# Splitting the weights of an encoder kernel by two GpSimd DMAs instead of by ScalarE and VectorE

## The chip, the core and the metric

The kernel runs on one core of a Trainium2 chip. TensorE (PE in the profile) multiplies matrices out of SBUF into PSUM; VectorE (DVE), ScalarE (ACT) and GpSimd (POOL) work elementwise; SyncE (SP) issues transfers between HBM and SBUF, and GpSimd can issue them as well. Each engine works through its own queue in order and waits on semaphores that other engines and transfers raise. The metric is the device time of one launch in microseconds; lower is better.

## What is computed

One inference step of a hybrid encoder of two layers, for a prompt of 512 columns and a sample of 64, both with the same weights, in float32:

```python
for l in range(DEPTH):                                   # DEPTH = 2, D_MODEL = 1024, D_FF = 2816
    x = x + 0.5 * ((silu(h @ w_gate) * (h @ w_up)) @ w_down)     # h = rms_norm(x), first feed-forward
    u = rms_norm(x) @ w_in                               # three groups of heads: band, differential, latent
    x = x + concat(A, B, C) @ w_out                      # softmax mixers with per-head RMS norms
    x = x + memory_attention(rms_norm(x), k, v)          # k, v from 256 memory tokens: mem_w_k, mem_w_v
    x = x + 0.5 * ((silu(h @ w_gate) * (h @ w_up)) @ w_down)     # second feed-forward
```

The outputs are both groups' x and the new keys, values and latents of each layer.

## The kernel before

Activations stand transposed, 128 features by 576 columns (512 of the prompt and 64 of the sample), worked on in two halves of 288. To keep float32 accuracy with the fast matrix format, each operand is split into a rounded part, hi, and a remainder, lo = value - hi; a product is three matmuls, hi x hi, hi x lo and lo x hi. For the weights these parts are the tiles `whi` and `wlo`, 128 rows by up to 512 columns.

All weights lie in one array `wf` in the order of their use, cut into units of up to 1024 columns. `take` (line 575) fetches the next unit: `fetch` lets SyncE load it into a buffer `stage`, and `parts` splits it in pieces of 512 columns: `whi` is rounded by ScalarE or VectorE (`hi`, line 524), and `wlo` is `stage` less `whi` on VectorE (`split2`, line 543). `rows2` (line 596) takes two units at once for a form of seven products of half the size: of its seven weight operands three are `stage` itself and four are sums `wc` made of it, and all seven go through `parts`.

A feed-forward layer has 22 row tiles of gate and up. The first 4 run singly (tiles `g`, `u`), the others in pairs by `rows2` (products `P`); the down products (`d`) of a chunk of tiles stand amid the pairs of the next chunk, three, three and two of them behind each pair, and the last eight at the end. A down unit of six blocks is two weight tiles, of 512 and 256 columns. Then come the input projections (`pj`, `cq`, `ckv`, `uq`, `ukv`) mixed with attention (scores `S`, maps `p`, transposes `T`, outputs `O`), keys and values of the memory (`mk`, `mv`), the output projection (`wo`), the memory's queries (`mq`) and output (`mo`), and the second feed-forward layer.

The order of all this isn't written by hand. `Program` records every instruction with a cost per engine, `order` runs a list scheduler over them (per engine the instruction that can start first among the 24 of highest priority, within the buffers at hand), and `issue` (line 387) emits them; all instructions therefore have line 401 in the profile. An instruction that may run on several engines goes to the one that the planner's model finishes first on. The time of a matmul in that model is `n / 2.4 + 3` ns for n columns. Weights have a priority ahead of their use by up to 9.9 us (`ahead`). Buffers: 49 of 576 columns, 11 of 896, 3 stages, 6 each for `whi` and `wlo`.

Of the kernel before, what the change touches and what calls it, by code (L numbers as in the profile page):

```python
# [49 lines left out]
def ffn_steps():  # L50
    """Gate and up, the first row tiles singly and the others in pairs; the down products of a chunk amid the next one's."""
# [98 lines left out]
class Tile:  # L150
    """A tile of the recorded program; it gets its place when the ordered program is issued."""
# [68 lines left out]
class Op:  # L220
    __slots__ = ("calls", "costs", "prio", "deps", "users", "wait", "need", "tiles", "ends", "start", "extra", "done", "port")


class Program:
    """Records instructions, orders them by a model of the engines, then issues them in that order."""

    def __init__(self):
# [8 lines left out]
        self.reach = {"s": (-12000.0, 3000.0), "b": (-12000.0, 4000.0)}  # L236
# [6 lines left out]
    def op(self, costs, calls, outs, ins, extra=0.0):  # L243
        o = Op()
        sb = sum(1 for v in ins if isinstance(v, View) and v.tile.tag != "sm" and v.size() > 1)
# [29 lines left out]
    def order(self, slots, window=60000.0, depth=24):  # L275
# [43 lines left out]
        while len(out) < len(self.ops):  # L319
# [52 lines left out]
            if e == "SP":  # L372
                dma = max(end + 650.0, dma) + o.extra
                o.extra = dma + 900.0 - end
                end = dma + 900.0
# [44 lines left out]
class Trunk:  # L420
    N_S = 49
    N_B = 11
    STAGE = 3
    WB = 6
# [27 lines left out]
    def mms(self, items):  # L452
        """One uninterrupted run of matrix products: (out, lhsT, rhs, start, stop, transpose)."""
        cost, calls, outs, ins = 0.0, [], [], []
        for out, lhsT, rhs, start, stop, tr in items:
# [4 lines left out]
            elif rhs.dtype == F32:  # L460
                cost += 2 * max(2 * n / 2.4, 107) + 6
            else:
                cost += max(n / 2.4 + 3, 60 if lhsT is self.lastw else (107 if m > 64 else 60))
# [54 lines left out]
    def load(self, out, src):  # L518
        self.p.op({"SP": 475.0}, [("dma_start", dict(out=out, in_=src))], [out], [], out.size() * 4 * out.shape[0] / 360.0)

    def store(self, dst, src):
        self.p.op({"SP": 475.0}, [("dma_start", dict(out=dst, in_=src))], [], [src], src.size() * 4 * src.shape[0] / 360.0)
# [51 lines left out]

    def take(self):
        """The next unit of the weights: loaded, and split into two parts that one pass each carries."""
        p = self.p
        keep, p.shift = p.shift, self.ahead()
        st, u = self.fetch()
        n = UNIT_COLS[u]  # L580
        hl = [self.parts(st[:, c:min(n, c + 512)]) for c in range(0, n, 512)]
# [14 lines left out]
    def rows2(self):  # L596
        """Two row tiles of the next weights times self.xc in seven products of half the size (Winograd's form)."""
# [894 lines left out]
```

## Time and profile before

| what | value |
|---|---|
| median of 3 runs | 2457.14 us (2455.83 to 2457.31) |
| span of the profiled execution, first to last instruction | 2453.7 us |
| busy share of PE, VectorE, ScalarE, GpSimd | 99%, 81%, 54%, 8% |
| moved by DMA | 224.19 MB, of it 208.33 MB read from HBM |
| granted clock of TensorE, mean | 1.000 |

The profiled execution's time around its span is not listed; its span stands 3.4 us under the median of the runs. Matmuls are pipelined and their ends are modelled: one of 288 columns is shown as 0.29 us long while the next begins 0.13 us after it. So the busy share of PE says more than the engine does, and the number of matmuls in a stretch, or the distance of their starts, tells how full it is.

### The profile page before, as it was taken

What the parts mean: (1) busy time and instruction counts of PE and PEld (TensorE: products, weight loads), DVE (VectorE), ACT (ScalarE), POOL (GpSimd) and SP (SyncE); (2) the same over time, 40 slices, a digit from 0 to 9 for tenths busy, and PEclk for the clock granted to TensorE, in tenths of its full rate; (3) what the DMA queues carried; (4) which work ended last, traced back from release to release, by engine and by line L of the source; (5) the groups of instructions that cost most, each with busy time, mean ns of one, the idle gap of its engine ahead of it and who ended that gap; (6) DMA issues with size and microseconds to landing.
All of it is one profiled execution on the core that took longest, in us unless ns stands there. A gap on an engine that the chain in (4) does not pass through costs nothing.

```text
span 2453.7 us, 46432 instructions
## 1 busy us (share of the span) xinstructions
PE 2427.7 (99%) x18150; PEld 2392.1 (97%) x18150; DVE 1978.0 (81%) x4044; ACT 1326.7 (54%) x2682; POOL 202.9 (8%) x187
## 2 busy tenths in 40 slices
PE   8999999999999999999999999999999999999999
PEld 8999999999989999999999999999999999999999
DVE  8987776689886898887688877776898868987774
ACT  6544445679765644443454444465897556444442
POOL 1000000022020010000020000000211101100000
PEclk9999999999999999999999999999999999999999
DMA  4232233122332123222323232331223421223322
GB/s 146 95 98 82 89 110 121 63 72 76 117 126 74 52 83 99 90 81 93 100 70 99 85 102 82 111 114 61 74 93 104 130 69 62 78 93 93 93 82 94
DMA packets 77452, 224.19 MB, mean 91 GB/s; under 512 B 8880, under 2 KB 13040, under 8 KB 77232
## 3 DMA queue, kind: packets, MB, share of 16 engines
q1 hardware_dynamic: 77232, 221.23, 27.8%
q8 instruction: 142, 2.33, 0.4%
q14 instruction: 78, 0.64, 0.1%
HBM read 208.33 MB, written 12.86 MB: 90 GB/s over the span
## 4 chain that ended last, share of the span: by engine, by line
PE 92%; DVE 5%; ACT 2%; issue 1%; DMA 0%; SPq 0%; DVEq 0%; ACTq 0%
PE P L401 32%; PE d L401 23%; PE pj L401 7%; PE wo L401 4%; PE g L401 4%; PE u L401 4%; PE mq L401 2%; PE mo L401 2%; PE O L401 2%; PE st L401 2%; PE cq L401 2%; DVE p L401 1%; PE ckv L401 1%; PE S L401 1%; PE T L401 1%; PE OS L401 1%
## 5 line engine op out<-in xcount | busy, mean ns | idle before, releaser
L401 ACT ACTIVATE whi<-stage 128x512 fp32r<-128x512 f32 (+1 forms) x609 | 362.9, 597 | 502.9 <-PE P L401 188.5
L401 DVE TENSOR_TENSOR wlo<-stage,whi 128x512 fp32r<-128x512 f32 (+1 forms) x706 | 460.8, 662 | 130.5 <-ACT whi L401 113.4
L401 PE MATMUL d<-hhi,wlo 128*128 128x288 f32 x1408 | 415.0, 295 | 0.0
L401 PE MATMUL d<-hhi,whi 128*128 128x288 f32 x1408 | 414.9, 295 | 0.0
L401 PE MATMUL d<-hlo,whi 128*128 128x288 f32 x1408 | 414.7, 295 | 0.0
L401 ACT ACTIVATE whi<-wc 128x512 fp32r<-128x512 f32 x284 | 179.4, 633 | 327.3 <-PE d L401 171.2
L401 DVE TENSOR_TENSOR wlo<-wc,whi 128x512 fp32r<-128x512 f32 x288 | 198.3, 690 | 91.4 <-ACT whi L401 87.3
L401 PEld LDWEIGHTS d<-hhi,wlo 128*128 128x128 f32 x1408 | 264.1, 188 | 0.0
L401 PEld LDWEIGHTS d<-hhi,whi 128*128 128x128 f32 x1408 | 264.1, 188 | 0.0
L401 PEld LDWEIGHTS d<-hlo,whi 128*128 128x128 f32 x1408 | 264.1, 188 | 0.0
L401 PE MATMUL P<-xbl,whi 128*128 128x288 f32 x864 | 254.2, 294 | 0.4 <-DVE xbl L401 0.4
L401 PE MATMUL P<-xbh,wlo 128*128 128x288 f32 x864 | 254.5, 295 | 0.0
L401 PE MATMUL P<-xbh,whi 128*128 128x288 f32 x864 | 254.0, 294 | 0.0
L401 PE MATMUL pj<-xhi,whi 128*128 128x288 f32 x576 | 172.0, 299 | 0.0
L401 PE MATMUL P<-xsl,whi 128*128 128x288 f32 x576 | 169.7, 295 | 0.6 <-DVE xsl L401 0.6
L401 PE MATMUL P<-xsh,wlo 128*128 128x288 f32 x576 | 169.7, 295 | 0.1
L401 PE MATMUL P<-xrh,wlo 128*128 128x288 f32 x576 | 169.8, 295 | 0.0
L401 PE MATMUL pj<-xhi,wlo 128*128 128x288 f32 x576 | 169.8, 295 | 0.0
L401 PE MATMUL P<-xrl,whi 128*128 128x288 f32 x576 | 169.7, 295 | 0.0
L401 PE MATMUL P<-xsh,whi 128*128 128x288 f32 x576 | 169.7, 295 | 0.0
L401 PE MATMUL pj<-xlo,whi 128*128 128x288 f32 x576 | 169.6, 295 | 0.0
L401 PE MATMUL P<-xrh,whi 128*128 128x288 f32 x576 | 169.6, 294 | 0.0
(415 smaller groups left out, 6897.5 us busy)
## 6 DMA issues: line engine op xcount, KB each, us to landing
stage<-wf SPq DMA_DIRECT2D x269, 512.0 KB, 3.5
stage<-wf SPq DMA_DIRECT2D x100, 384.0 KB, 3.0
stage<-wf SPq DMA_DIRECT2D x40, 256.0 KB, 2.7
o_k<-ev SPq DMA_DIRECT2D x12, 288.0 KB, 2.1
o_v<-ev SPq DMA_DIRECT2D x12, 288.0 KB, 2.7
cache<-ckv SPq DMA_DIRECT2D x12, 256.0 KB, 3.9
x<-x SPq DMA_DIRECT2D x8, 288.0 KB, 5.7
o_y<-x SPq DMA_DIRECT2D x8, 288.0 KB, 2.1
```

The lines of the kernel that those rows point to most:

```text
L401: getattr(eng[e], fn)(**{n: real(v) for n, v in k.items()})
```

## The change

Weights outside the seven-product form (all but the very first unit, which keeps the old path) are no longer staged. GpSimd issues a DMA from `wf` into `whi`, which rounds on the way because the target is the fast format (`cast`); ScalarE writes the negative of `whi` into `wlo`; and GpSimd issues a second DMA from the same place of `wf`, which adds to `wlo` (`gather`). So each such weight is read from HBM twice, and VectorE has no part in it. 388 tiles of 512 and 100 of 256 columns go this way; the 216 `stage` operands of `rows2` and its 288 `wc` stay. The priority of a cast is 3 us further ahead than that of the rest of its unit.

With it come other numbers: 8 instead of 6 buffers each for `whi` and `wlo`, 2 instead of 3 stages, 47 instead of 49 general buffers; a limit on how early the tags `hi` and `lo` may be taken; 2048 instead of 256 bytes for the descriptors of GpSimd's DMAs; and the planner's matmul cost, now `0.4375 * n + 7`, 133 ns for 288 columns where it was 123. All engines' orders are made anew by that.

```diff
-        self.reach = {"s": (-12000.0, 3000.0), "b": (-12000.0, 4000.0)}
+        self.reach = {"hi": (0.0, 4500.0), "lo": (0.0, 4500.0), "s": (-12000.0, 3000.0), "b": (-12000.0, 4000.0)}
...
-    N_S = 49
+    N_S = 47
     N_B = 11
-    STAGE = 3
-    WB = 6
+    STAGE = 2
+    WB = 8
...
-                cost += max(n / 2.4 + 3, 60 if lhsT is self.lastw else (107 if m > 64 else 60))
+                cost += max(0.4375 * n + 7, 60 if lhsT is self.lastw else (109 if m > 64 else 60))
...
+    def cast(self, out, src):
+
+        self.p.op({"POOL": 1000.0}, [("dma_start", dict(out=out, in_=src))], [out], [], out.size() * 4 * out.shape[0] / 360.0, True)
+
+    def gather(self, out, src):
+
+        self.p.op({"POOL": 1000.0}, [("dma_start", dict(out=out, in_=src, accum_op=ALU.add))], [out], [out],
+                  out.size() * 8 * out.shape[0] / 360.0, True)
...
+    def loaded_parts(self, src, n):
+
+        hi, lo = self.new("hi", [128, 512], F32R, "whi"), self.new("lo", [128, 512], F32R, "wlo")
+        self.p.shift -= self.EARLY
+        self.cast(hi[:, :n], src)
+        self.p.shift += self.EARLY
+        self.act(lo[:, :n], hi[:, :n], AF.Copy, scale=-1.0)
+        self.gather(lo[:, :n], src)
+        return hi, lo
+
+    EARLY = 3000.0
+
...
-        st, u = self.fetch()
-        n = UNIT_COLS[u]
-        hl = [self.parts(st[:, c:min(n, c + 512)]) for c in range(0, n, 512)]
+        u = self.unit
+        if u:
+            self.unit += 1
+            n = UNIT_COLS[u]
+            src = self.a["wf"][int(UNIT_OFF[u]):int(UNIT_OFF[u + 1])].rearrange("(p c) -> p c", p=128)
+            hl = [self.loaded_parts(src[:, c:min(n, c + 512)], min(n - c, 512)) for c in range(0, n, 512)]
+        else:
+            st, u = self.fetch()
+            n = UNIT_COLS[u]
+            hl = [self.parts(st[:, c:min(n, c + 512)]) for c in range(0, n, 512)]
...
-    nc = _bacc.Bacc("TRN2", target_bir_lowering=False, num_devices=1, dynamic_dma_scratch_size=256)
+    nc = _bacc.Bacc("TRN2", target_bir_lowering=False, num_devices=1, dynamic_dma_scratch_size=2048)
```

Three places show how the orders move. The first is ScalarE at the start of the program, before (`x_66` is the first tile of x):

```order
L401 ACT_TABLE_LOAD
L401 ACTIVATE accsq<-x_66 128x576
L401 ACTIVATE xhi<-x_66,gains 128x576
L401 ACTIVATE xhi<-x_74,gains 128x576
L401 ACTIVATE sq<-x_74 128x576
```

And ScalarE at the same place after the change (`x_68` is the first tile of x):

```order
L402 ACT_TABLE_LOAD
L402 ACTIVATE wlo<-whi 128x512
L402 ACTIVATE accsq<-x_68 128x576
L402 ACTIVATE xhi<-x_68,gains 128x576
L402 ACTIVATE wlo<-whi 128x512
```

Two negations of weights now stand around the first work on x; each waits for a cast to land.

The second is the queue that loads weights amid the pairs and down products of the first feed-forward layer: SyncE's before (1024 columns are a unit of `rows2`, 512 and 768 a down unit).

```order
L401 DMA stage<-wf 128x1024
L401 DMA stage<-wf 128x512 x3
L401 DMA stage<-wf 128x1024 x4
L401 DMA stage<-wf 128x512 x3
L401 DMA stage<-wf 128x1024 x4
```

GpSimd's queue there after the change, casts (`whi`) and additions (`wlo`):

```order
L402 DMA whi<-wf 128x512
L402 DMA wlo<-wf 128x512
L402 DMA whi<-wf 128x512 x2
L402 DMA wlo<-wf 128x512 x2
L402 DMA whi<-wf 128x512 x3
L402 DMA wlo<-wf 128x512 x3
L402 DMA whi<-wf 128x512 x2
L402 DMA wlo<-wf 128x512 x2
L402 TENSOR_TENSOR wc<-stage 128x512
```

The down units' loads have moved from SyncE to GpSimd, two for each tile, and an addition stands behind all the casts of its group; SyncE keeps the units of `rows2`.

The third is VectorE amid attention in the first layer, behind the split of a sample's transposed map (`ptsl`), before:

```order
L401 TENSOR_TENSOR ptsl<-TS,pts 64x128
L401 TENSOR_TENSOR ptsl<-TS,pts 128x256
L401 TENSOR_TENSOR ev<-pj,rb 128x288
L401 SCALAR_TENSOR_TENSOR ev<-ev,gains,sqf 128x576
L401 TENSOR_TENSOR vlo<-cache,vhi 128x256
L401 TENSOR_TENSOR qlo<-ev,qhi 128x576
L401 COPY qbd_769<-qhi 64x64
L401 COPY qbd_771<-qlo 64x64 x2
L401 TENSOR_TENSOR wlo<-stage,whi 128x512
L401 SCALAR_TENSOR_TENSOR ev<-ev,gains,sqf 128x576
L401 TENSOR_TENSOR ev<-pj,rb 128x288
L401 TENSOR_TENSOR wlo<-stage,whi 128x512
```

VectorE at a like place after the change:

```order
L402 TENSOR_TENSOR ptsl<-TS,pts 64x128
L402 TENSOR_TENSOR ptsl<-TS,pts 128x256
L402 TENSOR_TENSOR sql<-sqf,sqh 128x576
L402 TENSOR_TENSOR vlo<-cache,vhi 128x256
L402 SCALAR_TENSOR_TENSOR ev<-ev,gains,sqf 128x576
L402 TENSOR_TENSOR qlo<-ev,qhi 128x576
L402 TENSOR_TENSOR ev<-pj,rb 128x288
L402 COPY qbd_724<-qlo 64x64 x2
L402 TENSOR_TENSOR ev<-pj,rb 128x288
L402 TENSOR_TENSOR sqf<-ev 128x576
```

The subtractions of weights have gone from the queue, and squares and their remainders (`sqf`, `sql`), which ScalarE or GpSimd had in part before, stand there instead.

## Rows read from the trace of the kernel before

**Rows 1.** The page's first part: busy time and share of each engine.

```profile
span 2453.7 us, 46432 instructions
...
PE 2427.7 (99%) x18150; PEld 2392.1 (97%) x18150; DVE 1978.0 (81%) x4044; ACT 1326.7 (54%) x2682; POOL 202.9 (8%) x187
```

**Rows 2.** The page's fourth part, the chain that ended last: shares by engine.

```profile
PE 92%; DVE 5%; ACT 2%; issue 1%; DMA 0%; SPq 0%; DVEq 0%; ACTq 0%
```

**Rows 3.** Timeline, start and end: start, length, instruction, idle time before it.

```profile
5.55 0.43 DVE L401 CAST whi<-stage 128x512 fp32r<-128x512 f32 x1 [4.55 <-DMA stage<-wf]
...
6.13 0.58 PE L401 MATMUL g<-xhi,whi 128*128 128x288 f32 x1 [6.13 <-DVE whi L401]
...
2449.72 0.29 PE L401 MATMUL d<-hhi,wlo 128*128 128x288 f32 x1
```

**Rows 4.** Table of stretches: engines' busy us (instructions), TensorE's clock, DMA share.

```profile
50.00:100.00 50.00, 48.88 (x365) 48.18 (x364) 48.98 (x99) 24.92 (x45) 6.10 (x10) 1.00 0.30 94
100.00:150.00 50.00, 50.00 (x380) 50.00 (x378) 41.89 (x79) 23.30 (x41) 0.00 (x0) 1.00 0.31 101
400.00:450.00 50.00, 50.00 (x373) 48.82 (x372) 34.59 (x90) 32.89 (x74) 4.44 (x6) 1.00 0.28 96
...
500.00:700.00 200.00, 193.85 (x1417) 182.15 (x1416) 182.34 (x481) 168.29 (x408) 41.16 (x42) 1.00 0.28 93
1750.00:1950.00 200.00, 193.85 (x1454) 184.22 (x1454) 184.04 (x489) 159.93 (x398) 43.41 (x40) 1.00 0.31 102
```

**Rows 5.** TensorE's waits (its weight loads): releaser, us in total, times, longest.

```profile
PEld T L401 <- DVE p L401: 4.6, 7, 0.8
...
PEld st L401 <- DVE sql L401: 3.3, 10, 0.7
PEld TS L401 <- ACT ps L401: 2.7, 5, 1.1
```

**Rows 6.** Timeline of TensorE in attention, one stop.

```profile
518.11 0.30 PE L401 MATMUL st<-sqh,onesr 96*96 96x288 f32 x1
518.86 0.38 PE L401 MATMUL st<-sql,onesr 96*96 96x288 f32 x1 [0.45 <-DVE sql L401]
```

**Rows 7.** Groups by shape: busy us, mean ns of one | idle.

```profile
L401 DVE TENSOR_TENSOR wlo<-stage,whi 128x512 fp32r<-128x512 f32 x606 | 421.0, 702 | 114.6 <-ACT whi L401 97.6
...
L401 ACT ACTIVATE whi<-stage 128x512 fp32r<-128x512 f32 x511 | 321.9, 631 | 433.0 <-PE P L401 129.6 <-issue 99.9 <-PE d L401 55.9
...
L401 DVE CAST whi<-stage 128x512 fp32r<-128x512 f32 x95 | 42.7, 452 | 19.6 <-PE pj L401 7.7 <-DMA stage<-wf 4.5 <-PE mq L401 3.5
L401 DVE TENSOR_TENSOR wlo<-stage,whi 128x256 fp32r<-128x256 f32 x100 | 42.1, 421 | 15.8 <-ACT whi L401 15.8
...
L401 POOL CAST cqs<-qhi 128x64 fp32r<-128x64 f32 x4 | 8.0, 1989 | 11.0 <-ACT qhi L401 11.0
```

**Rows 8.** Stretches again, instructions on wlo alone, then on whi or wlo.

```profile
500.00:700.00 200.00, 85.89 (x291) 53.65 (x290) 29.38 (x41) 1.00 0.28 93
...
50.00:100.00 50.00, 48.64 (x244) 38.87 (x242) 16.83 (x25) 14.05 (x23) 1.00 0.30 94
500.00:700.00 200.00, 119.11 (x582) 92.46 (x582) 37.76 (x59) 14.57 (x24) 1.00 0.28 93
```

**Rows 9.** DMA: MB and share of 16 engines; issues, KB, median us to landing.

```profile
q1 hardware_dynamic: 77232, 221.23, 27.8%
...
stage<-wf SPq DMA_DIRECT2D x40, 256.0 KB, 2.7
...
cache<-ckv SPq DMA_DIRECT2D x12, 256.0 KB, 3.9
x<-x SPq DMA_DIRECT2D x8, 288.0 KB, 5.7
...
cst<-cckv SPq DMA_DIRECT2D x2, 256.0 KB, 5.9
```

**Rows 10.** Chain from 695 to 705 us: start, length, instructions.

```profile
701.39 3.24 PE mv L401 x27
```

## What I expect of the change

> **What bounds the kernel now.** I read the page's busy shares first. TensorE (PE) is busy 2427.7 of 2453.7 us, VectorE 81%, ScalarE 54%, GpSimd 8% [rows 1]; the chain of work that ended last is 92% PE [rows 2]. So whatever is taken off the vector engines is worth something only where PE waits for them. Span less PE busy is 26.0 us. 6.1 of that is the wait before the first matmul [rows 3], and 3.7 lies behind the last one, which ends at 2450.0 [rows 3], while the output is stored; 16.2 us are waits inside. Next, the table of stretches [rows 4]: from 100 to 150 us, in the feed-forward layer, PE is full, 380 matmuls in 50 us or 131.6 ns each. The stretch from 50 to 100 us holds 365, with VectorE at 48.98 of 50. The two attention stretches, 500 to 700 and 1750 to 1950 us, show PE at 193.85 of 200 each, so 12.3 of the 16.2 us are there; VectorE is at 182 to 184 and ScalarE at 160 to 168 of 200. The list of PE's waits names softmax maps and squares late from VectorE or ScalarE first, no weight tile among its longest [rows 5]. A wait also costs more than it shows, since matmul ends are modelled: in [rows 6] two matmuls start 0.75 us apart where 0.13 would do, so 0.62 us is lost and 0.45 is shown. The hidden 0.17 us comes with each stop, and stops are mostly 0.3 to 1.1 us, so I take the true loss inside at up to twice the shown one, some 30 us. That is the ceiling of any gain inside.
>
> **What VectorE and ScalarE lose and get.** Counted in the two orders, 488 weight tiles (388 of 512 columns, 100 of 256) leave the old path. VectorE loses 388 subtractions at 702 ns and 100 at 421 ns [rows 7], 272.4 + 42.1 = 314.5 us, and 91 of 95 roundings at 452 ns, 41 us. The planner gives it back some of GpSimd's work (28 sums of wc, at about the 702 ns of a subtraction 20 us, and a few smaller), so VectorE should end near 1978 - 315 - 41 + 30 = 1650 us, 67%. ScalarE no longer rounds 297 wide and 98 narrow tiles, but negates all 488: 91 wide ones more at 631 ns [rows 7], about +58 us, near 56%. PE's matmuls are the same in number and shape. In the saturated stretches all of this is worth nothing.
>
> **Where PE waits, what it is worth.** From 500 to 700 us VectorE spends 29.4 us on weights' low parts and another 8.4 us on roundings (the row of whi or wlo less that of wlo) [rows 8]. There VectorE and ScalarE together go from 350.6 of 400 us to 350.6 - 37.8 + 11.7 (some 18 negations more at 631 ns) = 324.5, so their free time grows from 49 to 75 us, by half. If waits for a late vector engine fall as its queue has half again as much room, a third of them goes: of 24.6 us in both attention stretches (12.3 shown, doubled) 8 us. From below this could be 0 (the waits are the length of the softmax chain itself, which is not shortened), from above all 24.6. I take 8, since the longest waits in [rows 5] are of both sorts. From 50 to 100 us, 15 matmuls are missing, 15 x 0.1316 = 2.0 us, behind a VectorE that is full, with 16.8 us of it on low parts [rows 8]: gone, -2. From 400 to 450 us 7 matmuls are missing [rows 4], 0.9 us, and the 50 us behind it lack as many, beside the first work of attention: -2, with 0 as the other end.
>
> **The start.** ScalarE's second instruction is now a negation that waits for the first cast. Before, the first matmul at 6.13 waits for the rounding of the first tile, which begins at 5.55 [rows 3]. A cast issued at about 0.8 us and landing as the 256 KB loads do, in 2.7 to 5.9 us [rows 9], is there at 3.5 to 6.7; negation, square and scaled x (some 0.65 each, 2.1 in all) then end at 5.6 to 8.8 against 6.13: a delay of 0 to 2.7 us. Five casts and three additions also share the DMA engines with x, whose loads already take 5.7 us [rows 9]. I take +2, with 0 and +5 as ends.
>
> **The chain that has to stay hidden.** A weight tile now needs cast, negation, addition in turn, and each waits on the one before. No row shows a GpSimd DMA. Each leg is bounded below by 2.7 us (256 KB loads of SP beside little else) and above by 5.9 (the slowest such load) [rows 9]; the addition also reads its target, so its upper end is twice that, 11.8. With a negation of 0.63 the chain is 6.0 to 18.3 us. I take 3.9 (the median of the loads amid attention) + 0.63 + 5.3 = 9.8. It is covered by eight slots: a cast can go out when PE frees the slot eight tiles back, and seven tiles of PE work stand between. Where a run of products P gives way to down products, those seven are 12 matmuls each, 7 x 12 x 0.1316 = 11.1 us; counted in the new order, the 224 down tiles have 11.4 to 21 us. 9.8 is within it, by little, so it costs nothing. One rule speaks here: the Trainium skill (DMA: Bandwidth & Descriptors, Anatomy of one DMA) gives a GpSimd DMA about 2.0 us plus its bytes at 436 GB/s, 2.6 us for 256 KB; by it the chain would be about 6 to 7 us and the sum unchanged. No run shows that yet.
>
> GpSimd's own queue has 976 DMAs. In-order, an addition that waits for ScalarE holds the later casts, and PE waits for those. The tightest place is memory keys, memory values and output projection: 32 tiles, 64 DMAs, against 16 x 12 x 0.120 us (27 matmuls in 3.24) [rows 10] + 16 x 24 x 0.1316 = 73.5 us of PE, and a lead of seven wide tiles, 22 us, so 95 us in all: 1.5 us for each DMA. GpSimd's slowest elementwise row is 2.0 us [rows 7], the upper end, nothing the lower; I take 1.0, the middle, since no tile passes through the engine here, which fits. The DMA engines: 221 MB took 27.8% [rows 9], so 256 KB takes 0.81 us of them; a cast plus an addition at twice that is 2.4 us, where PE uses a 512-column tile in 3.16. It fits as well, and would not if the addition ran at a third of the copy's rate.
>
> **Sum.** -8 - 2 - 2 + 2 = -10 us. The profiled execution has a span of 2453.7, and its launch adds what lies around; the median of the runs is 2457.1, 3.4 more, so I use that: 2447 us.
>
> **Rivals.** (1) No change: the waits are latency of softmax, squares and norms, and an emptier VectorE does not shorten them. For it: PE waits for maps that have only just been made [rows 5]; against: VectorE at 91% there. Time 2452 to 2462.
> (2) Slower: additions land late. It decides at a chain of 11.1 us. Each feed-forward layer changes from products to down products at nine places, 36 in all; a chain of 13 us stops PE 1.9 us at each, 68 us: 2457 - 10 + 68 = 2515. At the far end, 18.3 us, 36 x 7.2 = 259 us more. For it: loads of 256 KB already take up to 5.9 us, and traffic grows; against: the median of plain ones is 2.7.
> (3) Slower: GpSimd's issue is the bound. It decides at 1.5 us per DMA. At 2.0 us, the upper end above, the place above needs 128 us against 95, 33 us per layer, and the last eight down units of each feed-forward layer 64 us against 38 + 21, 5 us each: 66 + 20, so 2533. The Trainium skill (SBUF — State Buffer, SBUF: two separate sides) says that VectorE in its two-port copy mode locks GpSimd out and that descriptors then cannot be written; that would be this rival's cause. Of such instructions (casts, copies, scalings) the order counts 240 before and 192 after, so there are fewer and not more.
>
> **Chances.** The forecast 0.48 (its own range 2426, with all 24.6 us gained in attention, to 2452), no change 0.15, late additions 0.22, GpSimd's issue 0.15. A change of 0.2%, 4.9 us, is about what a measurement here can tell from none; so faster 0.48, same 0.15, slower 0.37. The range runs from 2426 to 2515: above it lie the worse halves of both slower cases, below it almost nothing.
>
> **What would show it.** Right: VectorE near 67%, PE over 195 of 200 in both attention stretches, 380 matmuls per 50 us still in the feed-forward layers, no wait of PE for whi or wlo among its longest. Wrong by (2): PE waiting for a DMA into wlo at the first matmul of down products. Wrong by (3): GpSimd's DMAs without a pause from 690 to 770 us while PE stands. By (1): the same waits for p, ps and sql in the same sizes. A first matmul after 8 us would refute the start's term.

## The result and the profile after

The changed kernel takes 2515.53 us (median; 2513.99 to 2519.51) against 2456.48 us beside it: a ratio of 1.0243, 95% interval 1.023 to 1.0256. It is 59 us slower. The prediction had said 2447 with a range up to 2515; the direction was wrong and the time lies just outside. Rival (2), additions that land late, had 2515 as its time, but that is a coincidence: the place it named is not where the time went.

The page after: span, and busy time of each engine.

```profile
span 2515.1 us, 47479 instructions
...
PE 2451.7 (97%) x18150; PEld 2400.5 (95%) x18150; DVE 1700.5 (68%) x3594; ACT 1336.8 (53%) x2722; POOL 796.7 (32%) x1085
```

Against [rows 1], VectorE is as empty as forecast (68%, forecast 67%), and PE's 18150 matmuls are the same in number. The chain that ended last is no longer PE's alone:

```profile
PE 70%; issue 11%; POOL 6%; ACT 5%; DMA 5%; DVE 3%; SPq 0%; POOLq 0%; ACTq 0%; DVEq 0%
```

It was 92% PE [rows 2]; now GpSimd, ScalarE and transfers hold 16%. The table of stretches of the changed kernel (columns as in [rows 4]: PE, weight loads, VectorE, ScalarE, GpSimd, clock, DMA share, GB/s):

```profile
0.00:50.00 50.00, 39.14 (x240) 37.26 (x241) 36.36 (x60) 29.70 (x47) 22.91 (x33) 0.93 0.82 204
...
50.00:100.00 50.00, 50.00 (x381) 50.00 (x380) 40.20 (x84) 23.88 (x45) 10.90 (x18) 1.00 0.49 115
100.00:150.00 50.00, 50.00 (x382) 50.00 (x381) 38.98 (x75) 21.64 (x39) 6.10 (x9) 1.00 0.45 125
...
500.00:700.00 200.00, 187.93 (x1312) 174.05 (x1310) 149.18 (x403) 155.77 (x366) 61.58 (x88) 0.98 0.55 123
1750.00:1950.00 200.00, 187.15 (x1316) 173.76 (x1315) 150.51 (x411) 157.45 (x370) 63.43 (x88) 0.98 0.56 124
...
720.00:770.00 50.00, 44.10 (x316) 42.76 (x316) 21.48 (x44) 24.70 (x47) 26.93 (x39) 0.93 1.00 232
```

The feed-forward layer is full (382 matmuls in 50 us, 380 before), and from 50 to 100 us PE does 381 where it did 365 [rows 4]. The loss is elsewhere: in the attention stretches PE starts 1312 and 1316 matmuls where it started 1417 and 1454 [rows 4], although VectorE has a quarter of its time free there. (The same stretch of the clock does not hold quite the same work in both kernels; the table by parts below does.) The last row is the other kind of place: amid memory values and the output projection VectorE and ScalarE are half idle and GpSimd too, but the 16 DMA engines are busy all the time (share 1.00) though they move only 232 GB/s, and PE starts 316 matmuls. At the start of the kernel before, the same share had moved 391 GB/s:

```profile
10.00:15.00 5.00, 5.00 (x31) 5.00 (x30) 5.00 (x9) 5.00 (x10) 0.00 (x0) 1.00 1.00 391
```

So it is the engines' time that is used up, and not a rate in bytes. From 720 to 770 us, the kernel before reads:

```profile
720.00:770.00 50.00, 50.00 (x379) 50.00 (x378) 31.30 (x51) 20.67 (x32) 0.00 (x0) 1.00 0.30 95
```

Where the 61.4 us between the two spans arise is read from the timelines, by the start of the first matmul of each part (us; `pj` opens attention, `mk` the memory keys, `g` the second feed-forward layer):

| | g | pj | mk | g | pj, layer 2 | mk | g | end of span |
|---|---|---|---|---|---|---|---|---|
| before | 6.1 | 403.8 | 673.1 | 839.6 | 1623.7 | 1893.0 | 2057.5 | 2453.7 |
| after | 8.5 | 408.9 | 697.7 | 872.7 | 1656.8 | 1944.8 | 2118.8 | 2515.1 |
| lost in the part ahead | 2.4 | 2.7 | 19.6 | 8.5 | 0.0 | 18.7 | 9.5 | 0.1 |

So 5 us go at the start, 38.3 in the two attention stretches (288.8 and 288.0 us long, 269.3 before), 18.0 from memory to the second feed-forward layer, and nothing in the feed-forward layers behind that. PE's longest waits after:

```profile
PEld g L402 <- ACT xhi L402: 12.8, 5, 8.5
PEld st L402 <- DVE sql L402: 12.5, 21, 1.2
PEld T L402 <- DVE p L402: 9.2, 10, 1.9
PEld pj L402 <- DMA wlo<-wf: 6.4, 3, 2.8
PEld wo L402 <- DMA wlo<-wf: 4.6, 2, 2.6
...
PEld d L402 <- DMA wlo<-wf: 1.3, 4, 0.7
```

(Each row: what waits, and for what; us in total, times, longest.) Additions into `wlo` are waited for at `pj` and `wo`, hardly at down products `d`, where rival (2) had put them; and waits for `sql` and `p` are 12.5 and 9.2 us where they were 3.3 and 4.6 [rows 5]. The DMA queues after (packets, MB, share of 16 engines; issues, KB, median us to landing):

```profile
q0 software_dynamic: 140544, 229.70, 46.7%
q1 hardware_dynamic: 39360, 106.39, 13.2%
...
whi<-wf POOLq DMA_DIRECT2D x388, 256.0 KB, 5.2
wlo<-wf POOLq DMA_DIRECT2D x388, 256.0 KB, 4.6
...
x<-x SPq DMA_DIRECT2D x8, 288.0 KB, 10.2
```

GpSimd's queue takes 46.7% of 2515.1 us, 1175 us of all 16 engines for 438 times 256 KB (388 + 100/2): 2.68 us for a cast and its addition. SyncE's plain 256 KB took 0.81 us [rows 9]. The loads of x at the start land in 10.2 us instead of 5.7.

### The profile page after: what moved, and what is told of

It is laid out like the page before. It is cut to its first block, busy times and chain, and to the rows that moved or that the text cites. A ratio compares the mean times of both kernels' runs of the same rounds, so it can differ in the third digit from the quotient of the medians.

```text
span 2515.1 us, 47479 instructions
## 1 busy us (share of the span) xinstructions
PE 2451.7 (97%) x18150; PEld 2400.5 (95%) x18150; DVE 1700.5 (68%) x3594; ACT 1336.8 (53%) x2722; POOL 796.7 (32%) x1085
## 3 DMA queue, kind: packets, MB, share of 16 engines
q0 software_dynamic: 140544, 229.70, 46.7%
## 4 chain that ended last, share of the span: by engine, by line
PE 70%; issue 11%; POOL 6%; ACT 5%; DMA 5%; DVE 3%; SPq 0%; POOLq 0%; ACTq 0%; DVEq 0%
PE P L402 30%; PE d L402 20%; PE u L402 4%; PE g L402 4%; DMA whi<-wf 3%; POOL wlo L402 3%; PE pj L402 3%; POOL whi L402 3%; PE wo L402 2%; PE cq L402 1%; DMA wlo<-wf 1%; ACT sqf L402 1%; PE ckv L402 1%; ACT p L402 1%; PE st L402 1%
## 5 line engine op out<-in xcount | busy, mean ns | idle before, releaser
L402 POOL DMA_DIRECT2D wlo<-wf x488 | 442.1, 974 | 815.9 <-ACT wlo L402 604.9
L402 POOL DMA_DIRECT2D whi<-wf x488 | 355.0, 821 | 703.7 <-PE P L402 513.5
L402 ACT ACTIVATE wlo<-whi 128x512 fp32r<-128x512 f32 (+1 forms) x488 | 281.1, 587 | 452.3 <-DMA whi<-wf 372.3
L402 ACT ACTIVATE whi<-stage 128x512 fp32r<-128x512 f32 x214 | 132.6, 627 | 155.1 <-DMA stage<-wf 65.4
L402 DVE SCALAR_TENSOR_TENSOR x<-d,x 128x288 f32<-128x288 f32 x256 | 114.0, 453 | 101.1 <-PE d L402 100.9
L402 DVE TENSOR_TENSOR wlo<-stage,whi 128x512 fp32r<-128x512 f32 x218 | 148.6, 695 | 40.3 <-ACT whi L402 39.4
## 6 DMA issues: line engine op xcount, KB each, us to landing
o_k<-ev SPq DMA_DIRECT2D x12, 288.0 KB, 4.2
o_v<-ev SPq DMA_DIRECT2D x12, 288.0 KB, 5.9
```

What stands on the lines that cost most here:

```text
L402: getattr(eng[e], fn)(**{n: real(v) for n, v in k.items()})
```

## The experiments

Three theories stood at the outset. **Full DMA engines**: a cast and an addition take 2.7 us of all 16 engines, and where PE uses a tile faster than that, everything that moves is late. **Casts hold ScalarE**: negations wait in ScalarE's queue for casts, and softmax stands behind them. **Order**: the new numbers of the planner put squares and maps where PE waits for them, whatever the DMAs do. Rivals (2), the chain's latency, and (3), GpSimd's issue, came along. All kernels are compared with the kernel before on the same chip.

**Without the additions** (the order of all engines kept):

```diff
             for fn, k in o.calls[e] if isinstance(o.calls, dict) else o.calls:
+                if "accum_op" in k:
+                    continue
```

> The order of every engine stays that of the changed kernel, but the 488 additions are not issued; the remainders of those weights are then only the negated rounded parts, so the product is left incomplete. It is the ceiling of what the additions cost by any way: their time on the DMA engines, GpSimd's 442 us of issuing them, TensorE's waits for them. Theory 'full DMA engines': in memory keys, values and output projection (DMA share 0.91 from 700 to 800 us) the 18.6 us lost in both layers come back, with 4 us at the start and the 6 us of waits for additions at pj: about 2487. Theory 'order' (the planner's new numbers put sums and squares later, no matter what the DMAs do): the 38 us lost in the two attention stretches stay, so no less than 2480 and VectorE's squares (sql) stay the longest wait. Theory 'casts hold ScalarE' (negations wait for casts and what stands behind them is late): attention gets better only as far as casts land sooner, 2475 to 2490, ScalarE's 372 us of waiting for casts at least a third less. If the attention stretches come back as well and the time is near 2455, the additions are the whole cause.

Measured: 2474.22 us, 1.0074 (1.0059 to 1.0089). Of the 59 us, 41 go with the additions, a little more than any of the three theories had given them; 18 stay.

**Additions of 16 columns** separate bytes from issue and waiting:

```diff
+                if "accum_op" in k:
+                    k = dict(k, out=k["out"][:, :16], in_=k["in_"][:, :16])
```

> The same order again, each addition issued at its place with its waits, but for 16 columns of 512 or 256 (the other columns' remainders are left incomplete). Issue time and waiting chain stay, the bytes go. 'Full DMA engines': as without additions, within 5 us. 'GpSimd issue' (rival 3): it stays at 2505 to 2515. 'Late chain' (rival 2, latency of the last leg whatever its size): halfway at best, 2495 to 2510.

Measured: 2470.63 us, 1.006 (1.0043 to 1.0077). All 488 additions are issued, in their places, at 991 ns each, and the time is that of no additions. So what the additions cost is the time that their bytes take on the DMA engines: not the issue, and not a last leg that is late whatever its size, as the expectation put rival (2). (Smaller additions also land sooner, in 2.5 us where it was 4.6; the next run bears on that.) From 720 to 770 us, this kernel:

```profile
720.00:770.00 50.00, 49.48 (x380) 49.28 (x379) 17.28 (x31) 20.12 (x34) 26.68 (x36) 1.00 0.51 124
```

The DMA share falls from 1.00 to 0.51 and PE is full. Part by part, the bytes had cost 3.9 us before the first `pj`, 7.7 and 7.3 in the attention stretches (281.2 and 280.6 us now), 11.3 and 13.1 from memory to the next feed-forward layer, 2.2 and 0.7 behind that: 46 us between the spans. Of the 15 us left, 23 are in attention, and 8 are gains elsewhere.

**Half of the columns**:

```diff
+                if "accum_op" in k:
+                    n = k["out"].size() // 2
+                    k = dict(k, out=k["out"][:, :n], in_=k["in_"][:, :n])
```

> The changed kernel's order, every addition for the first half of its columns (the other half's remainders are left incomplete): a tile's cast and addition then take about 1.0 + 0.85 = 1.8 us of the DMA engines by the queue's share of time, against 2.7 in full and 1.3 with 16 columns. Theory 'full DMA engines' (a threshold: only where a stretch asks for more than all of the engines' time is something lost): most comes back, 2471 to 2482, and no 50 us at memory keys and values have a share near 1. Rival 'latency of the last leg' (each addition's landing counts, anywhere): in the middle, 2488 to 2498.

Measured: 2479.1 us, 1.0093 (1.0076 to 1.011). Half the bytes cost 8 us over the run with 16 columns, the other half 36 more. The cost is not by the byte: it rises where the engines fill up. From 705 to 765 us casts and additions land in 4.8 and 4.3 us here, about midway between the changed kernel (7.1 and 7.0) and the one with 16 columns (3.9 and 2.9), so a cost that grew with each landing would have put the time near the middle. From 700 to 750 us:

```profile
700.00:750.00 50.00, 45.84 (x355) 44.57 (x353) 27.05 (x57) 30.23 (x65) 30.33 (x42) 1.00 0.86 197
```

That is 355 matmuls, where 312 run with all columns (share 1.03; the shares of two queues add) and 372 with 16 (0.62).

**Additions in halves of 64 rows**, same bytes, more issues:

```diff
-        self.p.op({"POOL": 1000.0}, [("dma_start", dict(out=out, in_=src, accum_op=ALU.add))], [out], [out],
+        self.p.op({"POOL": 1000.0}, [("dma_start", dict(out=out[s], in_=src[s], accum_op=ALU.add)) for s in (slice(0, 64), slice(64, 128))], [out], [out],
```

> Each addition as two of 64 rows with the same row length: same bytes, 488 more issues of 0.97 us on GpSimd. 'GpSimd issue': the place with 32 tiles has 32 more issues, 31 us per layer, so 2560 to 2580. 'Full DMA engines': 2515 to 2525, since GpSimd has 68% of its time free and the bytes are the same.

The planner still counts one issue for each pair of halves, so the order is that of the changed kernel.

Measured: 2581.02 us, 1.0512 (1.0483 to 1.0541), the time that the issue theory had asked for, and 1 us more. GpSimd's groups (busy us, mean ns of one) in this kernel:

```profile
L402 POOL DMA_DIRECT2D wlo<-wf x976 | 849.0, 1328 | 644.7 <-ACT wlo L402 622.7 <-ACT p L402 6.6 <-ACT whi L402 4.7
L402 POOL DMA_DIRECT2D whi<-wf x488 | 488.9, 1238 | 595.4 <-PE P L402 467.2 <-DVE wlo L402 48.3 <-DVE c L402 30.2
```

A record is longer on the mean, 1.33 and 1.24 us where it was 0.97 and 0.82, but records overlap: 976 of 1.33 us would be 1296 us and fill 849. All issues of weights together, GpSimd's time in the changed kernel and in this one:

```profile
0.00:2600.00 2600.00, 708.50 (x976) 0.99 0.58 130
```

```profile
0.00:2600.00 2600.00, 1107.07 (x1464) 0.99 0.60 130
```

That is 0.73 and 0.76 us for each, so an issue is hardly longer; there are more of them. The time on the DMA engines stays nearly the same, 46.6% of 2588.7 us or 1206 for 1175. It costs in every part: attention 300.7 us, and 14.0 us in the feed-forward layers between, which had lost nothing. There PE now waits at the down products:

```profile
PEld d L402 <- issue: 14.9, 18, 2.9
```

So issue was not what the change lost by (the run with 16 columns has all of it), but it is the next limit: with one more issue in each chain PE stops at the down products in spite of eight buffers.

**Memory and output the old way**:

```diff
-        if u:
+        if u and PLAN[u][0] not in ("mem_w_k", "mem_w_v", "w_out", "mem_w_q", "mem_w_o"):
```

> The weights of memory keys, values, queries and output and of the output projection go the old way (load by SyncE, split by ScalarE and VectorE); all else as in the changed kernel, planned anew. 'Full DMA engines': the DMA share there falls under 0.5 and 15 to 20 us come back: 2495 to 2500, and the attention stretches up to the first memory keys stay as they are. 'Order' or 'casts hold ScalarE': within 6 us of 2515, as ScalarE and VectorE get these weights' work back.

Measured: 2499.31 us, 1.0178 (1.0163 to 1.0193), 16 us back, as full DMA engines had it: from memory to the next feed-forward layer it loses 1.7 and -1.1 us, where it was 8.5 and 9.5. (The orders are made anew here, as in all runs below that change a path or a number of the planner.) In the stretch that was saturated:

```profile
720.00:770.00 50.00, 49.41 (x389) 49.08 (x388) 38.98 (x74) 26.30 (x57) 4.12 (x2) 1.00 0.43 131
```

**Neither additions nor ScalarE's wait for casts**:

```diff
+                if fn == "dma_start" and isinstance(k["out"], View) and k["out"].tile.name == "rope":
+                    self.still = k["out"]
+                if fn == "activation" and k["in_"].tile.name == "whi" and hasattr(self, "still"):
+                    k = dict(k, in_=self.still[:, :k["in_"].size()])
```

> As the run without additions (2474.2), but ScalarE's negations read a constant tile in place of the rounded weight, in the same place of its queue and of the same length (all but the first ones, ahead of the constant's load); so ScalarE no longer waits for casts, 208 us there, and TensorE alone waits for them. The remainders of these weights hold no part of the weight, so the product is left incomplete. Theory 'casts hold ScalarE': the 12 us that each attention stretch loses without additions (281.2 against 269.3 us from the first projection to the first memory key) come back: 2448 to 2454. Theory 'order' (the planner's numbers put squares and maps where TensorE waits for them): the stretches stay at 278 to 282 us each, and the time at 2470 to 2476.

Measured: 2471.58 us, 1.0063 (1.0048 to 1.0078), within 3 us of the run without additions; attention stays at 281.1 and 280.8 us, and PE's longest waits are the same:

```profile
PEld T L408 <- DVE p L408: 10.0, 11, 1.9
PEld st L408 <- DVE sql L408: 9.5, 15, 1.2
```

"Casts hold ScalarE" falls for all but the first weights, which this run could not spare the wait: the rest of ScalarE's 208 us of waiting costs 3 us at most.

**The planner's numbers in the kernel before**, without any DMA of GpSimd. First the matmul cost alone:

```diff
-                cost += max(n / 2.4 + 3, 60 if lhsT is self.lastw else (107 if m > 64 else 60))
+                cost += max(0.4375 * n + 7, 60 if lhsT is self.lastw else (109 if m > 64 else 60))
```

> The kernel before with one number of the change, the planner's cost of a matmul (133 instead of 123 ns for 288 columns); no GpSimd DMA. Theory 'order by the new cost': each attention stretch gets some 12 us longer, 2475 to 2482, and TensorE waits longer for sql and p. Theory 'casts hold ScalarE', or anything else that needs the DMAs: 2450 to 2460, the attention stretches at 267 to 272 us.

Measured: 2461.02 us, 1.002 (1.001 to 1.0029): 5 us, far from the 19 to 26 that the theory had asked for. Then 47 general buffers with it:

```diff
-    N_S = 49
+    N_S = 47
```

> The kernel before with the change's matmul cost and its 47 general buffers in place of 49; no GpSimd DMA. It asks what the 12 us are that each attention stretch (first projection to first memory key) loses even when the additions move next to nothing: 281 us against 269; the cost number alone made 272 of it. Theory 'fewer buffers': 278 to 283 us, 2474 to 2482. Theory 'the new order of VectorE and ScalarE that goes with the DMA path': 270 to 274 us, 2458 to 2465.

Measured: 2464.7 us, 1.0031 (1.002 to 1.0043); attention 272.9 and 272.6 us, so the fewer buffers are not it either. And the limit on weight buffers on top:

```diff
-        self.reach = {"s": (-12000.0, 3000.0), "b": (-12000.0, 4000.0)}
+        self.reach = {"hi": (0.0, 4500.0), "lo": (0.0, 4500.0), "s": (-12000.0, 3000.0), "b": (-12000.0, 4000.0)}
```

> The kernel before with the new cost, 47 general buffers (2464.7) and the change's limit on how early weight buffers are taken; no GpSimd DMA. If the limit makes the attention stretches longer: 278 us or more each, 2475 to 2482. If not: 2460 to 2468.

Measured: 2486.66 us, 1.0127 (1.011 to 1.0144): 30 us lost with no DMA of GpSimd. Attention is 281.1 and 280.5 us long, as in the changed kernel with small additions, and PE waits for the same two tiles as in the changed kernel:

```profile
PEld st L401 <- DVE sql L401: 7.8, 14, 0.8
PEld T L401 <- DVE p L401: 7.3, 8, 1.5
```

The planner moved squares onto VectorE as in the changed kernel (`sqf` from `ev` there 21 times, 23 in the changed kernel, 8 before). That count alone doesn't make the stretch long: the last two runs below have 20 and 17, with attention at 266 to 271 us. The limit binds harder here, since it counts free buffers and there are six instead of eight. In the changed kernel it was doubled:

```diff
-        self.reach = {"hi": (0.0, 4500.0), "lo": (0.0, 4500.0), "s": (-12000.0, 3000.0), "b": (-12000.0, 4000.0)}
+        self.reach = {"hi": (0.0, 9000.0), "lo": (0.0, 9000.0), "s": (-12000.0, 3000.0), "b": (-12000.0, 4000.0)}
```

> The changed kernel with the limit on how early weight buffers may be taken at 9 us for each free one instead of 4.5. If the limit makes what attention loses without the additions' bytes (8 of 12 us in each stretch): 280 to 283 us per stretch and 2495 to 2503. If it does so only where there are six buffers (the kernel before): within 5 us of 2515. The bytes stay, so memory and output stay 9 us late per layer.

Measured: 2543.12 us, 1.0355 (1.0333 to 1.0376), slower still and outside both ranges, with attention at 301.9 and 297.6 us. So the number is not bad or good by itself: each value makes another order. Doubled, it makes attention 13 and 10 us longer here, and 3 and 5 us shorter in the last run below.

**Which weights go by DMA.** Only the feed-forward layers', with cost and stages of before and seven weight buffers of each kind:

```diff
-        if u:
+        if u and PLAN[u][0].startswith("ffn"):
...
-                cost += max(0.4375 * n + 7, 60 if lhsT is self.lastw else (109 if m > 64 else 60))
+                cost += max(n / 2.4 + 3, 60 if lhsT is self.lastw else (107 if m > 64 else 60))
...
-    STAGE = 2
-    WB = 8
+    STAGE = 3
+    WB = 7
```

> Only the feed-forward layers' single weights are split by GpSimd's DMAs; projections, memory and output go the old way, with the matmul cost of before, three stages and 7 + 7 weight buffers (47 general ones). Theory 'full DMA engines' with 'order': all that was lost behind 405 us is back, the start keeps its 2.5 to 5 us, and the steady stretches keep their gain (760 matmuls in 100 us against 757, some 1.5 us in each feed-forward layer of 400 us): 2450 to 2458. Rival: the loss in attention comes from the smaller number of buffers (47 for 49): the attention stretches stay at 275 to 282 us, 2470 or more.

Measured: 2489.18 us, 1.0136 (1.0119 to 1.0153); with the new cost, `N_S = 48`, `STAGE = 3` and `WB = 6`:

> As the run before it, with the new matmul cost, 48 general and 6 + 6 weight buffers. Theory 'order by the new cost': the attention stretches 10 to 12 us longer each than in the run before it, 2472 to 2480. If the cost number does nothing: 2450 to 2460 as that run.

Measured: 2538.89 us, 1.0345 (1.0323 to 1.0368). Neither was foreseen: PE now waits for additions in the feed-forward layers, at the place of rival (2). Its waits at the down products, with seven buffers and with six:

```profile
PEld d L402 <- DMA wlo<-wf: 16.7, 26, 1.4
```

```profile
PEld d L402 <- DMA wlo<-wf: 43.3, 54, 3.3
```

With eight it was 1.3 us. Each buffer less is one tile less of cover. With six, the feed-forward layers lose 46 us in all; with seven these waits are 17 of 33 us, and the rest isn't taken apart. The same units with all numbers of the change, eight buffers among them (the first line of that diff alone):

> All numbers of the changed kernel (cost, 47 general, 8 + 8 weight buffers, 2 stages, the limit on them); only the feed-forward layers' single weights are split by GpSimd's DMAs, the others go the old way through the two stages. If the loss in attention comes with loading its weights by GpSimd: stretches of 269 to 275 us and 2455 to 2466. If it comes with the planner's numbers or any new order: 278 to 284 us and 2472 to 2485. No stop at the down products beyond the changed kernel's 1.3 us (eight buffers).

Measured: 2480.01 us, 1.0096 (1.0081 to 1.0111). No stops at the down products (1.2 us); attention, whose weights now go the old way, is still 278.1 and 277.3 us. And the opposite, only the projections into attention the old way:

```diff
-        if u:
+        if u and PLAN[u][0] not in ("w_in", "c_w_uq", "c_w_ukv"):
```

> All numbers of the changed kernel; only the projections into attention (w_in and the latent ones) go the old way, memory, output and feed-forward weights by GpSimd's DMAs. 'Full DMA engines': the 7.5 us that additions' bytes cost in each attention stretch come back, the 9.5 us per layer in memory and output stay: 2498 to 2503; the other 12 us per stretch come back as well if they go with the path (2475 to 2482), and stay if they go with the numbers (2496 to 2504).

Measured: 2498.85 us, 1.0168 (1.0153 to 1.0183): attention 278.3 and 278.1 us, and 10.1 and 10.0 us still lost behind it, up to the second feed-forward layer. Both agree: without loading attention's weights by GpSimd some 10 us per stretch come back, and 8 to 9 stay with the plan's numbers (the two stages, through which those weights then go, may have a part in that).

**The planner told of later landings** (0.5 us more for GpSimd's DMAs):

```diff
-                o.extra = dma + 900.0 - end
-                end = dma + 900.0
+                lat = 900.0 if e == "SP" else 1400.0
+                o.extra = dma + lat - end
+                end = dma + lat
```

> The changed kernel planned anew with one number other: the planner takes GpSimd's DMAs to land 0.5 us later (cast 3.8 and addition 4.5 us after the start of the issue, where 5.2 and 4.6 are the measured medians of 256 KB, and 3.3 and 4.0 were planned). Theory 'the plan is too hopeful about landings': negations stand later on ScalarE and additions are waited for less: 2495 to 2508. Theory 'full DMA engines': the bytes are the same, 2510 to 2520.

Measured: 2519.82 us, 1.0255 (1.0239 to 1.027). No help, as full DMA engines had it: the bytes are the same.

**Only the down products by DMA**, where the DMA engines have room. With the change's numbers:

```diff
-        if u:
+        if u and PLAN[u][0].endswith("w_down"):
```

> All numbers of the changed kernel; only the down products' weights by GpSimd's DMAs, 224 tiles of 512 and none of the start. 'Full DMA engines' and 'chain within eight buffers': start as before, 760 matmuls in 100 us of the feed-forward layers, 1.5 us gained in each; attention by its order 270 to 280: 2450 to 2470. Rival, stages: with two of them for all other weights the attention stretches and memory lose 5 us or more each, 2475 or more.

Measured: 2480.16 us, 1.0097 (1.0082 to 1.0112), the start back at 6.6 us, attention 279.3 us in both layers, as the rival of that expectation. With cost and stages of before:

```diff
-    N_S = 47
-    STAGE = 2
+    N_S = 46
+    STAGE = 3
...
-                cost += max(0.4375 * n + 7, 60 if lhsT is self.lastw else (109 if m > 64 else 60))
+                cost += max(n / 2.4 + 3, 60 if lhsT is self.lastw else (107 if m > 64 else 60))
```

> Only the down products' weights are split by GpSimd's DMAs, all others the old way; the matmul cost and the three stages of before, 8 + 8 weight buffers, 46 general ones. Theory 'the chain needs eight buffers': no stop at the down products as with 7 and 6 (16.7 and 43.3 us of waits for the addition), under 3 us of such waits; together with 'full DMA engines' the start, memory and output are as before: 2450 to 2460. Rival 'the chain is too long for any place without spare DMA time': over 10 us of waits for additions, 2470 or more. Rival 'fewer general buffers': attention 10 us longer per layer, 2470 to 2480.

Measured: 2465.62 us, 1.0039 (1.0024 to 1.0054); waits for additions at `d` 2.7 us, attention 269.3 and 271.0 us, and 6 us over what was expected. With the limit doubled, as above:

> Only the down products by DMA, with the matmul cost and three stages of before, 8 + 8 weight buffers, 46 general ones (2465.6 with the limit of 4.5 us) and a limit of 9 us. If the limit is what it loses: 2452 to 2458, attention at 269 us. If the loss is the smaller number of general buffers or any new order: 2461 to 2470.

Measured: 2458.08 us (2454.25 to 2468.11), 1.0008 (0.9996 to 1.0019): attention 266.2 and 265.9 us, shorter than before the change, but 13.3 us of waits at the down products. It is level with the kernel before, at the edge of the first range. No version that was run beats the kernel before.

## Why the prediction was wrong

**What bounds the kernel** held for the kernel before: in the feed-forward layers, where PE was full, an emptier VectorE brought next to nothing (382 matmuls in 50 us for 380).

**The step that failed** is the end of "The chain that has to stay hidden": a cast and an addition take 2.4 us of the DMA engines, PE uses a tile in 3.16, so it fits. The 2.4 was near (2.68 measured). The 3.16 was the rate of a 512-column tile with 24 matmuls of 288 columns. The memory's keys and values use a tile in 12 matmuls of 256 columns, 12 x 0.120 = 1.44 us when nothing stands between. The prediction had this very place, 32 tiles in 73.5 us of PE, but set only GpSimd's issue against it. Against the DMA engines, 32 x 2.4 = 77 us, more than PE's time before any other transfer is counted; measured, 32 x 2.68 = 86. Only the lead of 22 us, which the prediction granted to GpSimd's issue there, would have covered that, and the engines had little room to build it: they were at 0.81 of their time already as this place began.

```profile
670.00:710.00 40.00, 38.30 (x292) 35.72 (x290) 34.57 (x116) 35.69 (x93) 16.00 (x24) 1.00 0.81 205
```

Between 705 and 765 us the changed kernel issued 21 pairs (issues, KB, median us to landing):

```profile
whi<-wf POOLq DMA_DIRECT2D x21, 256.0 KB, 7.1
wlo<-wf POOLq DMA_DIRECT2D x21, 256.0 KB, 7.0
```

21 x 2.68 = 56 of 60 us, and SyncE's transfers come on top: the engines set the pace. A chain is then 7.1 + 0.63 + 7.0 = 14.7 us, longer than the 10.1 that seven tiles of 1.44 us cover. So the place that the prediction had asked about for the chain, the down products, held, and another did not.

Of the 46 us that the additions' bytes cost, 24 lie from memory to the next feed-forward layer and 15 in attention, where the mean share is only 0.58. There casts and additions come in bunches (0.86 from 595 to 600 us, below), and with half of the columns nearly all of the 15 came back (281.7 and 281.5 us). Whether PE meets full engines or the longer landing there isn't parted by these runs.

**The start** was sized about right, and yet refuted by the prediction's own sign: +2 with 5 as the end, and the first matmul at 8.50 us is 2.4 us late and past the 8. That part is the mechanism it named, and not the additions' bytes: the negation ahead of the scaled x waits for the first cast, and with small additions the first matmul comes even later, at 9.5.

```profile
6.58 0.63 ACT L402 ACTIVATE wlo<-whi 128x512 fp32r<-128x512 f32 x1 [4.56 <-DMA whi<-wf]
```

What it left out is behind that, where x lands in 10.2 us instead of 5.7 and PE starts fewer matmuls from 10 to 30 us, in the changed kernel and with small additions:

```profile
10.00:30.00 20.00, 17.89 (x87) 16.33 (x87) 14.93 (x21) 13.85 (x23) 6.53 (x8) 0.83 0.92 252
```

```profile
10.00:30.00 20.00, 18.83 (x113) 17.62 (x113) 17.89 (x27) 16.28 (x26) 8.03 (x10) 1.00 0.64 191
```

5.0 us were lost by the first `pj`; 3.9 of them are the bytes' by that run.

**The gain in attention** (-8 us) did not come; 38.3 us were lost there instead. More room on VectorE didn't shorten the waits: with small additions VectorE is at 209 of 295 us there instead of 246, and PE still starts fewer matmuls. Nor did the waits keep their size, as rival (1) had it; they grew. No run has the emptier VectorE with the order of before, so what it is worth by itself stays open. These rows, from 405 to 700 us, are of the kernel before, of the changed kernel, of the one with small additions, and of the kernel before with the three planner numbers:

```profile
405.00:700.00 295.00, 288.85 (x2121) 274.74 (x2120) 245.86 (x645) 226.75 (x544) 47.69 (x52) 1.00 0.26 87
```

```profile
405.00:700.00 295.00, 280.11 (x1987) 262.62 (x1985) 201.00 (x551) 213.29 (x499) 97.15 (x140) 0.99 0.58 128
```

```profile
405.00:700.00 295.00, 284.17 (x2050) 267.27 (x2049) 209.29 (x592) 220.56 (x529) 100.79 (x144) 0.99 0.34 85
```

```profile
405.00:700.00 295.00, 279.98 (x1997) 262.22 (x1995) 240.73 (x633) 210.97 (x509) 33.90 (x43) 0.99 0.24 79
```

2121, 1987, 2050 and 1997 matmuls. The prediction treated the planner's numbers as part of the DMA path and put them at nothing without a reason: the second step that failed. They were an edit of their own: in the kernel before, three of them cost 30 us without one DMA of GpSimd. How much of attention's 12 us without the bytes is due to which number in the changed kernel stays open; the limit alone, doubled, moved the stretch from 288.8 to 301.9 us.

**50 to 100 us** (-2) was right, 381 matmuls for 365, and swallowed by the start. **400 to 500 us** (-2) was not: 341 matmuls from 400 to 450 us where there were 373 [rows 4]. With small additions it is 374, so here too it is the bytes.

```profile
400.00:450.00 50.00, 47.18 (x341) 44.81 (x340) 29.31 (x82) 31.96 (x71) 18.18 (x25) 1.00 0.70 148
```

**The chain** was well sized where the prediction needed it. From 1000 to 1600 us, in the feed-forward layers of the changed kernel (issues, KB, median us to landing):

```profile
whi<-wf POOLq DMA_DIRECT2D x65, 256.0 KB, 4.0
wlo<-wf POOLq DMA_DIRECT2D x65, 256.0 KB, 4.4
```

With a negation of 0.63 between them that is 9.0 against the 9.8 of the prediction, and the cover of eight buffers held; seven and six showed its edge. By the Trainium skill (DMA: Bandwidth & Descriptors, Anatomy of one DMA) an estimate for 256 KB of a GpSimd DMA is 2.6 us. The trace does not agree for these two kinds: over all casts of the changed kernel, of both sizes, it has

```profile
DMA to landing us min/median/max: 2.2/4.8/10.1
```

and 7.1 as the median of 256 KB where the engines are full; without the additions, casts of 256 KB came down to 3.1.

**GpSimd's issue** was sized high if anything, 0.73 us of GpSimd's time each against 1.0, and small additions with all their issues lost none of the 46 us, so rival (3) did not decide.

**The clock** was in no term. After a stop TensorE's granted clock falls to its lower level, 1.2 GHz, for some us. In the changed kernel, around the 2.8 us wait for an addition that ends at 599.6 us:

```profile
595.00:600.00 5.00, 1.55 (x7) 0.93 (x6) 4.76 (x9) 5.00 (x12) 2.45 (x3) 0.85 0.86 187
600.00:605.00 5.00, 5.00 (x23) 5.00 (x23) 2.53 (x5) 3.04 (x7) 1.40 (x3) 0.50 0.03 6
605.00:610.00 5.00, 5.00 (x33) 4.72 (x33) 4.41 (x16) 3.84 (x13) 0.71 (x1) 0.96 0.32 51
```

Seven matmuls in the first 5 us, then 23 at a clock of 0.50 where 38 would do, 15 x 0.13 = 2 us more than the wait itself. Over the span the mean is 0.993 (1.000 before, 0.999 with small additions); 0.7% of 2515 us is at most 17.6 us of the loss that follows stops in this way.

## What to carry to other kernels

Set every resource against the fastest consumer, stage by stage: a DMA path that fits the average of a kernel (47% of the engines' time) can saturate the one stage that uses tiles twice as fast. Don't count on a lead there unless the stage ahead leaves room for it. Price DMAs that cast or add by time of the DMA engines, not by bytes, and ask what else moves there. And where a change carries new numbers for a scheduler, run those numbers alone on the old path first; here three of them, with the old path's six buffers, were half as dear as the whole change.

## What the runs showed of the hardware

For 256 KB, all 16 DMA engines were busy 0.81 us with a plain load, 0.99 with a cast and 1.69 with an addition. The cast's figure is GpSimd's queue without additions, over 438 times 256 KB:

```profile
q0 software_dynamic: 70272, 114.85, 17.5%
```

17.5% of 2472.6 us is 433 us; the addition's figure is the rest of the 1175, if casts take as long beside additions. An addition of 16 columns, a 32nd of a wide tile's bytes, still took 0.26 us (22.7% of 2468.9 us, less 433, over 488). An issue on GpSimd took 0.54 us when casts stood alone (261 us for 488), and 0.73 to 0.76 us of GpSimd's time with additions among them. An addition's record is 0.86 us at the least in the changed kernel, and the same with 16 columns; an issue behind it can begin before that one's record ends, so the mean length of a record says more than an issue costs.
